# A log-sum-exp kernel on one core: another place for the last column of rows, and a transpose ahead of the last store

## The chip, the cores and the metric

The kernel runs on one core of a Trainium2 chip. A core has five engines that run their own instruction streams and wait for each other through semaphores: TensorE (PE in the profile), VectorE (DVE), ScalarE (ACT), GpSimd (POOL) and SyncE (SP). Sixteen DMA engines carry data between the chip's memory and the on-chip memory, whose 128 partitions are the rows of every tile here. The metric is the time of one execution on the device in microseconds (us); lower is better. The times before are 161.47, 161.47 and 161.59 us, with a median of 161.47 us.

## The reference

The input `x` holds 32 x 512 rows of 1024 numbers in fp32, 64 MB in all. The output is one number for each of the 16,384 rows:

```
max_x = max(x, axis=-1)
out   = max_x + log(sum(exp(x - max_x), axis=-1))
```

The kernel leaves the maximum out: it computes log(sum(exp(x))) straight away, checks on the way that no sum has left the range in which this is exact enough, and has a second, slower path with the maximum for inputs that fail this check. With the input used here the second path is jumped over.

## The kernel before

**Layout.** The 16,384 rows are spread over the 128 partitions, 128 rows to each, so a partition has 128 "columns", one per row. The columns come from two regions of the input. Columns 0 to 111 (`W` = 112) are the first 14,336 rows, and each partition has 112 rows that follow one another (`x_rows`). Columns 112 to 127 are the last 2,048 rows, 16 following rows to a partition (`x_rest`). The output is cut in the same way (`out_rows`, `out_rest`), so the last store of a partition's results writes 16 numbers, or 64 bytes, to one place.

**Stages.** The list `LOADS` says how many columns each load brings and what is done with them. SyncE issues all loads (line 143) into a ring of 48 columns; the first is 16 columns long, and toward the end they get shorter, down to 0.53 and 0.47 of a column. ScalarE applies the exponential to every load as it lands (line 235). The sums over a row are made in three ways: VectorE alone reduces whole rows (line 246); or GpSimd adds the halves of rows (line 240) and VectorE reduces the result (line 177); or, for the last loads, VectorE adds the two halves of one row and accumulates the sum in one instruction (line 256). The very last column, `LAST` = 127, is done in two pieces, "Y" and "Z", on ScalarE alone, which takes the exponential and the sum in one instruction (line 209). VectorE copies the first piece's sum into `sumexp` (line 219).

**Results.** The logarithms are ScalarE's: columns 0 to 111 at line 275, while the last loads are still coming; columns 112 to 126 at line 288; column 127 at line 290, which takes the second piece's sum and adds the first piece's as a bias. All land in the tile `res`. SyncE stores columns 0 to 111 at line 285, once the last load but one has landed, and columns 112 to 127 at line 294, once line 290 is done. This last store counts the semaphore `stored` up by 16 when it has landed.

**The check.** VectorE compares the sums with a lower bound (line 299) and the last piece's inputs with a ceiling (line 310). TensorE adds the findings up into a single number `count` (the small matmuls of lines 166, 305, 307 and 315). VectorE turns this into a truth value, `fine` (line 317), which ScalarE and VectorE each read into a register (line 321). Both then branch around the second path (line 373 is behind it), and each of them counts `done` up by one. SyncE waits for both, clears the kernel's semaphores (line 376), and ends with an instruction that waits for `stored` (line 378).

**Order.** Everything is written out by hand. Each engine executes its instructions in program order and a wait holds back all that is behind it on that engine. For this change three queues matter: SyncE's (line 285, line 294, lines 374 to 378), ScalarE's (lines 209, 288, 290, 321) and VectorE's (lines 219, 299, 310, 317, 321).

Of the kernel before, what the change touches and what calls it, by code (L numbers as in the profile page):

```python
# [16 lines left out]
B = 16  # L17
LATE = 119
AHEAD = 1
FIRST = 512  # L20


# [32 lines left out]
def kernel(  # L55
# [5 lines left out]
    nc = tc.nc  # L61
# [4 lines left out]
    P = nc.NUM_PARTITIONS  # L66
    fp32 = mybir.dt.float32
    i32 = mybir.dt.int32
    AF = mybir.ActivationFunctionType
# [3 lines left out]
    x_flat = x.flatten_outer_dims()  # L73
    n, d = x_flat.shape
    assert n % P == 0
    NC = n // P
    H = d // 2
    W = NC - B
    LAST = NC - 1
    x_rows = x_flat[0 : P * W].rearrange("(p c) d -> p (c d)", p=P)  # L80
    x_rest = x_flat[P * W : n].rearrange("(p c) d -> p (c d)", p=P)
    out_flat = out.rearrange("a b -> (a b)")
    out_rows = out_flat[0 : P * W].rearrange("(p c) -> p c", p=P)
    out_rest = out_flat[P * W : n].rearrange("(p c) -> p c", p=P)

    def source(e0, size):
        assert e0 >= W * d or e0 + size <= W * d
        return x_rest[:, e0 - W * d : e0 - W * d + size] if e0 >= W * d else x_rows[:, e0 : e0 + size]

    loads = [  # L90
        (int(size * d), [(op[0], 0 if op[0] == "Y" else int(op[1:] or 1)) for op in ops.split()])
# [5 lines left out]
    def sbuf(name, cols, dtype=fp32, rows=P):  # L97
        return nc.alloc_sbuf_tensor(name, [rows, cols], dtype).ap()

    ring = sbuf("ring", RING * d)  # L100
    sumexp = sbuf("sumexp", NC)
    res = sbuf("res", NC)
    clamped = sbuf("clamped", NC)
    bad = sbuf("bad", 3)
    over = sbuf("over", d)
# [7 lines left out]
    last_sum = nc.alloc_psum_tensor("last_sum", [P, 1], fp32).ap()  # L113
# [3 lines left out]
    act = Counted(nc, nc.scalar, "act")  # L117
    dve = Counted(nc, nc.vector, "dve")
    pe = Counted(nc, nc.tensor, "pe")
    pool = Counted(nc, nc.gpsimd, "pool")  # L120
    sp = Counted(nc, nc.sync, "early_store")
    done = nc.alloc_semaphore("done")
    again = nc.alloc_semaphore("again")
    ready = nc.alloc_semaphore("ready")
    stored = nc.alloc_semaphore("stored")
# [4 lines left out]
    dve.did(nc.vector.memset(steep, STEEP))  # L130
    less_at = dve.did(nc.vector.memset(less, -CEILING * (loads[-1][0] // 2)))


    users = []

    def load(i, here, done_before, size):
        for a, b, who, at in users:
            if a < here + size and b > here:
                sp.wait(who, at)
        users[:] = [u for u in users if not (u[0] < here + size and u[1] > here)]  # L140
        parts = [(0, FIRST), (FIRST, size)] if i == 0 else [(0, size)]
        return [
            nc.sync.dma_start(
                out=ring[:, here + a : here + b], in_=source(done_before + a, b - a)
            ).then_inc(landed[i], 16)
            for a, b in parts
        ]
# [36 lines left out]
    c = 0  # L184
    p = 0
# [6 lines left out]
    for i, (size, ops) in enumerate(loads):  # L192
        if here + size > RING * d:
            assert here == p
            p = here = 0
        if any(q < here + size and q + t * d > here for _, t, q, _ in folded):
            reduce_folded()
        dma = load(i, here, done_before, size)
        if i < AHEAD:
            first_loads.extend(x.ins for x in dma)  # L200
# [3 lines left out]
        for k, (how, s) in enumerate(ops):  # L204
            rows = ring[:, p : p + s * d].rearrange("p (c d) -> p c d", d=d)
            if how in "YZ":
# [3 lines left out]
                    out=last_exp[:, here - p : end - p], in_=ring[:, here:end], func=AF.Exp,  # L210
# [10 lines left out]
            elif how == "A":  # L221
# [3 lines left out]
                    out=v, in_=v, func=AF.Exp, accum_out=sumexp[:, c : c + 1]  # L225
# [11 lines left out]
            if how == "F":  # L237
# [3 lines left out]
                    out=rows[:, :, 0:H], in0=rows[:, :, 0:H], in1=rows[:, :, H:d], op=ALU.add  # L241
                ))
                folded.append((c, s, p, at))
            elif how == "R":
                dve.wait(act, at)
                who = (dve, dve.did(nc.vector.reduce_sum(  # L246
                    out=sumexp[:, c : c + s], in_=rows, axis=AX.X
                )))
                users.append((p, p + s * d, *who))
            elif how == "T":  # L250
# [3 lines left out]
                for r in range(s):  # L254
                    lo = rows[:, r, 0:H]
                    who = (dve, dve.did(nc.vector.scalar_tensor_tensor(  # L256
                        out=lo, in0=lo, scalar=1.0, in1=rows[:, r, H:d],
# [13 lines left out]
            if c == LATE:  # L271
# [4 lines left out]
                    out=res[:, 0:W], in_=sumexp[:, 0:W], func=AF.Ln  # L276
# [9 lines left out]

    act.wait(dve, dve.n)
    act.did(nc.scalar.activation(out=res[:, W:LAST], in_=sumexp[:, W:LAST], func=AF.Ln))  # L288
    act.wait(act, summed_by_act)
    ln_last = act.did(nc.scalar.activation(  # L290
        out=res[:, LAST:NC], in_=last_sum, func=AF.Ln, bias=sumexp[:, LAST:NC]
    ))
    sp.wait(act, ln_last)
    nc.sync.dma_start(out=out_rest, in_=res[:, W:NC]).then_inc(stored, 16)

# [2 lines left out]
        out=clamped[:, LATE:NC], in0=sumexp[:, LATE:NC], scalar=LOW,  # L300
# [10 lines left out]
        out=over[:, 0:half], in0=last_piece[:, 0:half], scalar=CEILING,  # L311
        in1=last_piece[:, half : 2 * half], op0=ALU.max, op1=ALU.max, accum_out=bad[:, 2:3],
    ))
    pe.wait(dve, dve.n)
    at = pe.did(nc.tensor.matmul(count, lhsT=bad[:, 2:3], rhs=steep, start=False, stop=True))  # L315
    dve.wait(pe, at)
    at = dve.did(nc.vector.tensor_scalar(out=fine, in0=count, scalar1=HIGH, scalar2=None, op0=ALU.is_lt))  # L317
    act.wait(dve, at)
# [8 lines left out]
            read.then_inc(done, 1)  # L327
    with nc.If(all_fine < 1):

        nc.scalar.wait_ge(sp.sem, 16)  # L330
        nc.scalar.wait_ge(stored, 16)
        rows = 0
        steps = 0
        for c0 in range(0, NC, RING):
            s = min(RING, NC - c0)
            v = ring[:, 0 : s * d].rearrange("p (c d) -> p c d", d=d)
            neg = clamped[:, c0 : c0 + s]
            if c0:
                nc.scalar.wait_ge(ready, steps)
            edge = max(c0, min(W, c0 + s))  # L340
            for c1, c2 in ((c0, edge), (edge, c0 + s)):
                if c1 == c2:
                    continue
                nc.scalar.dma_start(
                    out=ring[:, (c1 - c0) * d : (c2 - c0) * d],
                    in_=source(c1 * d, (c2 - c1) * d),
                ).then_inc(again, 16)
                rows += 16
            nc.vector.wait_ge(again, rows)
            nc.vector.tensor_reduce(  # L350
                out=neg, in_=v, op=ALU.max, axis=AX.X, negate=True
            ).then_inc(ready, 1)
            nc.vector.wait_ge(ready, steps + 1)
            nc.vector.tensor_add(
                out=v, in0=v, in1=neg[:, :, None].to_broadcast([P, s, d])
            ).then_inc(ready, 1)
            nc.scalar.wait_ge(ready, steps + 2)
            nc.scalar.activation(out=v, in_=v, func=AF.Exp).then_inc(ready, 1)
            nc.vector.wait_ge(ready, steps + 3)
            nc.vector.reduce_sum(  # L360
                out=sumexp[:, c0 : c0 + s], in_=v, axis=AX.X
            ).then_inc(ready, 1)
            steps += 4
        nc.scalar.wait_ge(ready, steps)
        nc.scalar.activation(out=res, in_=sumexp[:, 0:NC], func=AF.Ln).then_inc(ready, 1)
        nc.vector.wait_ge(ready, steps + 1)
        nc.vector.tensor_sub(out=res, in0=res, in1=clamped).then_inc(ready, 1)
        nc.scalar.wait_ge(ready, steps + 2)
        nc.scalar.dma_start(out=out_rest, in_=res[:, W:NC]).then_inc(again, 16)
        nc.scalar.dma_start(out=out_rows, in_=res[:, 0:W]).then_inc(again, 16)  # L370
        nc.scalar.wait_ge(again, rows + 32)

    nc.scalar.sem_inc(done, 1)
    nc.sync.wait_ge(done, 2)
# [2 lines left out]
    kind = dict(sync_type="semaphore", id=stored.num, ant_name="stored")  # L377
    nc.sync.add_instruction(mybir.InstEventSemaphore(
        name=nc.get_next_instruction_name(), engine=mybir.EngineType.SP,
        sync_info=mybir.SyncInfo(  # L380
            on_wait=[mybir.SyncWait(wait_mode="sem-ge-imm", wait_value=16, **kind)],
            on_update=[mybir.SyncUpdate(update_mode="sem-sub-imm", update_value=16, **kind)],
        ),
    ))

# [47 lines left out]
```

## Time and profile before

| what | value |
|---|---|
| median of the three runs | 161.47 us |
| the profiled execution's own time | 161.57 us |
| its span, from the first to the last instruction of the kernel | 160.2 us |
| time of the profiled execution outside the span | 1.37 us |
| ScalarE busy | 114.5 us (71%) |
| VectorE busy | 114.3 us (71%) |
| DMA queue of SyncE, share of 16 engines | 97.8% |
| read from memory | 67.11 MB, mean 419 GB/s |

The time outside the span is what the launch adds around the kernel. The span is what the instructions of the kernel take, and a change inside it moves the time by as much as the last instruction moves. In the rows of the profile a line "L290 ACT ACTIVATE res<-last_sum" is ScalarE's instruction of line 290, which writes `res` and reads `last_sum`; names that end in q (SPq, ACTq, DVEq) are what an engine's sequencer does by itself, such as issuing a DMA, reading a register or branching. "To landing" is the time from the issue of a DMA to its last semaphore count.

### The profile page before, as it was taken

How to read it: one execution, taken by the hardware profiler on the slowest of the kernel's cores; microseconds unless marked ns; L12 is line 12 of the kernel's file. 1: busy time of each engine (PE TensorE's matmuls, PEld its weight loads, DVE VectorE, ACT ScalarE, POOL GpSimd, SP SyncE). 2: the span in 40 equal slices, each digit the busy share in tenths (PEclk: the TensorE clock that was granted, in tenths of full speed). 3: DMA queues.
4: the chain of work that ended last, by engine and by line, in shares of the span. 5: the costliest groups of instructions: out<-in, count | busy, mean ns of one | idle time of the engine just before them, and what ended most of it. 6: DMA issues, size and time to landing. Idle time of an engine off the chain costs nothing.

```text
span 160.2 us, 221 instructions
## 1 busy us (share of the span) xinstructions
PE 2.2 (1%) x26; PEld 1.1 (1%) x26; DVE 114.3 (71%) x59; ACT 114.5 (71%) x31; POOL 37.3 (23%) x11
## 2 busy tenths in 40 slices
PE   0000000000000000000000000000000000000022
PEld 0000000000000000000000000000000000000011
DVE  0000000009999499994999859959999999999996
ACT  3000059980799708995099949992999989799996
POOL 0000000000000000000000994690004969891000
DMA  9996996996996996997999999999999999999992
GB/s 319 507 460 301 507 524 262 524 524 262 524 524 262 524 524 262 524 474 311 483 442 442 442 425 409 409 409 471 423 414 417 458 409 399 444 412 428 415 408 97
DMA packets 3025, 67.18 MB, mean 419 GB/s; under 512 B 592, under 2 KB 720, under 8 KB 1488
## 3 DMA queue, kind: packets, MB, share of 16 engines
q1 hardware_dynamic: 3024, 67.18, 97.8%
q14 instruction: 1, 0.01, 0.0%
HBM read 67.11 MB, written 0.07 MB: 419 GB/s over the span
## 4 chain that ended last, share of the span: by engine, by line
DMA 51%; ACT 28%; DVE 19%; issue 1%; PE 0%
DMA ring<-in_x_dram 51%; ACT ring L235 28%; DVE sumexp L246 16%; DVE sumexp L177 2%; DVE ring L256 1%; DVE over L310 0%; PE count L315 0%; ACT res L275 0%; DVE clamped L299 0%; DVE fine L317 0%; DVE sumexp L219 0%
## 5 line engine op out<-in xcount | busy, mean ns | idle before, releaser
L235 ACT ACTIVATE ring<-ring 128x16384 f32<-128x16384 f32 (+16 forms) x23 | 111.7, 4908 | 42.3 <-DMA ring<-in_x_dram 42.3
L246 DVE TENSOR_REDUCE sumexp<-ring 128x16 f32<-128x16384 f32 (+4 forms) x9 | 85.6, 9513 | 42.1 <-ACT ring L235 42.1
L240 POOL TENSOR_TENSOR ring<-ring 128x3072 f32<-128x3072 f32 (+3 forms) x7 | 37.1, 5315 | 107.2 <-ACT ring L235 107.2
L177 DVE TENSOR_REDUCE sumexp<-ring 128x6 f32<-128x3072 f32 (+3 forms) x7 | 18.4, 2659 | 0.0
L256 DVE SCALAR_TENSOR_TENSOR ring<-ring 128x512 f32<-128x512 f32 x15 | 9.6, 687 | 0.4 <-ACT ring L235 0.4
L127 ACT ACT_TABLE_LOAD x1 | 1.3, 1283 | 1.9 <-PEq L64 1.9
L162 PE MATMUL count<-far,bad 128*1 128x1 f32 x2 | 0.2, 164 | 153.0 <-DVE clamped L157 153.0
L166 PE MATMUL count<-sumexp,ones 128*1 128x1 f32 x18 | 1.6, 164 | 3.6 <-DVE ring L256 3.6
L128 DVE MEMSET ones<- 128x1 f32 x1 | 0.1, 59 | 2.0 <-PEq L64 2.0
L256 DVE DVE_READ_ACCUMULATOR ring<-ring 128x1 f32 x15 | 1.2, 82 | 0.0
L209 ACT ACTIVATE last_exp<-ring 128x544 f32<-128x544 f32 (+1 forms) x2 | 1.2, 588 | 0.0
L162 PEld LDWEIGHTS count<-far,bad 128*1 128x1 f32 x2 | 0.1, 82 | 153.0 <-DVE clamped L157 153.0
L166 PEld LDWEIGHTS count<-sumexp,ones 128*1 128x1 f32 x18 | 0.8, 81 | 4.4 <-DVE ring L256 4.4
L310 DVE SCALAR_TENSOR_TENSOR over<-ring 128x240 f32<-128x240 f32 x1 | 0.4, 404 | 0.0
L317 DVE TENSOR_SCALAR fine<-count 1x1 int32<-1x1 f32 x1 | 0.1, 147 | 0.3 <-PE count L315 0.3
L157 DVE SCALAR_TENSOR_TENSOR clamped<-clamped,sumexp 128x119 f32<-128x119 f32 x1 | 0.3, 283 | 0.0
L275 ACT ACTIVATE res<-sumexp 128x112 f32<-128x112 f32 x1 | 0.3, 279 | 0.0
L290 ACT ACTIVATE res<-last_sum,sumexp 128x1 f32<-128x1 f32 x1 | 0.3, 261 | 0.0
L209 ACT ACTIVATION_READ_ACCUMULATOR last_exp<-ring 128x1 f32 x2 | 0.3, 129 | 0.0
L152 DVE TENSOR_SCALAR clamped<-sumexp 128x119 f32<-128x119 f32 x1 | 0.2, 222 | 0.0
L288 ACT ACTIVATE res<-sumexp 128x15 f32<-128x15 f32 x1 | 0.2, 213 | 0.0
L299 DVE SCALAR_TENSOR_TENSOR clamped<-sumexp 128x9 f32<-128x9 f32 x1 | 0.2, 170 | 0.0
(17 smaller groups left out, 1.8 us busy)
## 6 DMA issues: line engine op xcount, KB each, us to landing
ring<-in_x_dram SPq DMA_DIRECT2D x1, 7936.0 KB, 21.3
ring<-in_x_dram SPq DMA_DIRECT2D x1, 6912.0 KB, 23.9
ring<-in_x_dram SPq DMA_DIRECT2D x1, 6400.0 KB, 19.7
ring<-in_x_dram SPq DMA_DIRECT2D x1, 4608.0 KB, 15.9
ring<-in_x_dram SPq DMA_DIRECT2D x1, 3584.0 KB, 24.0
ring<-in_x_dram SPq DMA_DIRECT2D x1, 3072.0 KB, 19.1
ring<-in_x_dram SPq DMA_DIRECT2D x1, 2288.0 KB, 24.2
ring<-in_x_dram SPq DMA_DIRECT2D x1, 1664.0 KB, 20.9
```

The source lines that it names most:

```text
L127: nc.scalar.preload_act_table_set("natural_log_exp_and_others")
L157: dve.did(nc.vector.scalar_tensor_tensor(out=clamped[:, 0:LATE], in0=clamped[:, 0:LATE], scalar=0.0, in1=sumexp[:, 0:LATE], op0=ALU.bypass ...
L162: pe.did(nc.tensor.matmul(count, lhsT=bad[:, 0:1], rhs=far, start=True, stop=False))
L166: return pe.did(nc.tensor.matmul(count, lhsT=ones, rhs=sumexp[:, c : c + 1], **kw))
L177: at = dve.did(nc.vector.reduce_sum(out=sumexp[:, c0 : c0 + s0], in_=halves, axis=AX.X))
L209: at = act.did(nc.scalar.activation(out=last_exp[:, here - p : end - p], in_=ring[:, here:end], func=AF.Exp, accum_out=first_sum if how == ...
L235: at = act.did(nc.scalar.activation(out=v, in_=v, func=AF.Exp))
L240: at = pool.did(nc.gpsimd.tensor_tensor(out=rows[:, :, 0:H], in0=rows[:, :, 0:H], in1=rows[:, :, H:d], op=ALU.add))
L246: who = (dve, dve.did(nc.vector.reduce_sum(out=sumexp[:, c : c + s], in_=rows, axis=AX.X)))
L256: who = (dve, dve.did(nc.vector.scalar_tensor_tensor(out=lo, in0=lo, scalar=1.0, in1=rows[:, r, H:d], op0=ALU.mult, op1=ALU.add, accum_out ...
L275: ln_early = act.did(nc.scalar.activation(out=res[:, 0:W], in_=sumexp[:, 0:W], func=AF.Ln))
L310: dve.did(nc.vector.scalar_tensor_tensor(out=over[:, 0:half], in0=last_piece[:, 0:half], scalar=CEILING, in1=last_piece[:, half : 2 * half ...
```

## The change

The columns now come from three regions of the input. Columns 0 to 111 are where they were. Columns 112 to 126 are 15 following rows to each partition. Column 127 is the last 128 rows of the input, one for each partition, side by side (`x_last`). The loads keep their sizes; the two pieces of the last column now start 4 KB apart from partition to partition, where they were 64 KB apart, and the other pieces of the tail 60 KB.

The store at the end becomes two. The first, of columns 112 to 126, is 60 bytes from each of the 128 partitions; SyncE issues it after the logarithms of line 288. For column 127 the logarithm goes into the first column of a new tile `turn` (128 x 32), whose other columns GpSimd sets to zero at the start. VectorE then transposes each block of 32 x 32 into `turned`. Partitions 0, 32, 64 and 96 of `turned` now hold 32 results each in a row, and SyncE stores these four rows of 128 bytes. VectorE waits for line 290 before the transpose, which stands ahead of line 317 in its queue. `stored` counts to 32.

In the second path, which isn't executed here, the loads and stores follow the three regions, and two waits are moved from ScalarE to VectorE.

```
@@
+SQUARE = 32
@@
-    x_rest = x_flat[P * W : n].rearrange("(p c) d -> p (c d)", p=P)
+    x_rest = x_flat[P * W : P * LAST].rearrange("(p c) d -> p (c d)", p=P)
+    x_last = x_flat[P * LAST : n]
@@
-    out_rest = out_flat[P * W : n].rearrange("(p c) -> p c", p=P)
+    out_rest = out_flat[P * W : P * LAST].rearrange("(p c) -> p c", p=P)
+    out_last = out_flat[P * LAST : n]
 
     def source(e0, size):
-        assert e0 >= W * d or e0 + size <= W * d
-        return x_rest[:, e0 - W * d : e0 - W * d + size] if e0 >= W * d else x_rows[:, e0 : e0 + size]
+        for c0, c1, rows in ((0, W, x_rows), (W, LAST, x_rest), (LAST, NC, x_last)):
+            if c0 * d <= e0 < c1 * d:
+                assert e0 + size <= c1 * d
+                return rows[:, e0 - c0 * d : e0 - c0 * d + size]
@@
+    turn = sbuf("turn", SQUARE)
+    turned = sbuf("turned", SQUARE)
@@
+    pool.did(nc.gpsimd.memset(turn, 0.0))
@@
     act.did(nc.scalar.activation(out=res[:, W:LAST], in_=sumexp[:, W:LAST], func=AF.Ln))
+    sp.wait(act, act.n)
+    nc.sync.dma_start(out=out_rest, in_=res[:, W:LAST]).then_inc(stored, 16)
     act.wait(act, summed_by_act)
     ln_last = act.did(nc.scalar.activation(
-        out=res[:, LAST:NC], in_=last_sum, func=AF.Ln, bias=sumexp[:, LAST:NC]
+        out=turn[:, 0:1], in_=last_sum, func=AF.Ln, bias=sumexp[:, LAST:NC]
     ))
-    sp.wait(act, ln_last)
-    nc.sync.dma_start(out=out_rest, in_=res[:, W:NC]).then_inc(stored, 16)
@@
     at = pe.did(nc.tensor.matmul(count, lhsT=bad[:, 2:3], rhs=steep, start=False, stop=True))
+    dve.wait(act, ln_last)
+    row = dve.did(nc.vector.transpose(out=turned, in_=turn))
+    sp.wait(dve, row)
+    nc.sync.dma_start(
+        out=out_last.rearrange("(b q) -> b q", q=SQUARE), in_=turned[0:P:SQUARE, :]
+    ).then_inc(stored, 16)
     dve.wait(pe, at)
     at = dve.did(nc.vector.tensor_scalar(out=fine, in0=count, scalar1=HIGH, scalar2=None, op0=ALU.is_lt))
...
-            on_wait=[mybir.SyncWait(wait_mode="sem-ge-imm", wait_value=16, **kind)],
-            on_update=[mybir.SyncUpdate(update_mode="sem-sub-imm", update_value=16, **kind)],
+            on_wait=[mybir.SyncWait(wait_mode="sem-ge-imm", wait_value=32, **kind)],
+            on_update=[mybir.SyncUpdate(update_mode="sem-sub-imm", update_value=32, **kind)],
```

More of the change, by code (lines that the diff above doesn't have):

```diff
@@ L328 @@
     with nc.If(all_fine < 1):
-        nc.scalar.wait_ge(sp.sem, 16)
-        nc.scalar.wait_ge(stored, 16)
+        nc.vector.wait_ge(sp.sem, 16)
+        nc.vector.wait_ge(stored, 32)
         rows = 0
@@ L339 @@
                 nc.scalar.wait_ge(ready, steps)
-            edge = max(c0, min(W, c0 + s))
-            for c1, c2 in ((c0, edge), (edge, c0 + s)):
+            edges = [max(c0, min(e, c0 + s)) for e in (0, W, LAST, NC)]
+            for c1, c2 in zip(edges, edges[1:]):
                 if c1 == c2:
@@ L368 @@
         nc.scalar.wait_ge(ready, steps + 2)
-        nc.scalar.dma_start(out=out_rest, in_=res[:, W:NC]).then_inc(again, 16)
+        nc.scalar.dma_start(out=out_last[:, None], in_=res[:, LAST:NC]).then_inc(again, 16)
+        nc.scalar.dma_start(out=out_rest, in_=res[:, W:LAST]).then_inc(again, 16)
         nc.scalar.dma_start(out=out_rows, in_=res[:, 0:W]).then_inc(again, 16)
-        nc.scalar.wait_ge(again, rows + 32)
+        nc.scalar.wait_ge(again, rows + 48)
     nc.scalar.sem_inc(done, 1)
```

## The prediction

> **What bounds the kernel now.** I read the page's chain first, then SyncE's waits, and then the last four microseconds in order of time, because the change leaves the first 157 us alone but for the addresses of the tail's loads.
>
> ```profile
> span 160.2 us, 221 instructions
> ...
> DMA 51%; ACT 28%; DVE 19%; issue 1%; PE 0%
> ```
>
> The body is a stream of loads. The windows of the tail show how the DMA engines and ScalarE stand to each other there (the last two columns are the DMA share and GB/s):
>
> ```profile
> 80.00:100.00 20.00, 0.00 (x0) 0.00 (x0) 17.76 (x2) 17.61 (x3) 9.97 (x1) 1.00 1.00 433
> ...
> 138.00:142.00 4.00, 0.00 (x0) 0.00 (x0) 4.00 (x2) 3.94 (x3) 3.29 (x2) 1.00 0.99 426
> 142.00:146.00 4.00, 0.00 (x0) 0.00 (x0) 4.00 (x3) 4.00 (x2) 2.73 (x2) 1.00 0.99 423
> 146.00:150.00 4.00, 0.00 (x0) 0.00 (x0) 4.00 (x9) 4.00 (x2) 0.00 (x0) 1.00 0.99 418
> 150.00:154.00 4.00, 0.38 (x4) 0.17 (x4) 3.57 (x14) 4.00 (x4) 0.00 (x0) 1.00 1.00 413
> ```
>
> From 142 us on ScalarE is busy 4.00 of every 4.00 us and the DMA engines are too: the two are in step. A faster tail of loads would gain next to nothing, since ScalarE has no gap to close; a slower one would cost its loss in full. The end, from the last exponential on, in order of time:
>
> ```profile
> 157.25 0.61 ACT L209 ACTIVATE last_exp<-ring 128x544 f32<-128x544 f32 x1
> 157.26 0.35 SPq L285 DMA_DIRECT2D out_dram<-res  x1
> ...
> 157.99 0.15 DVE L219 COPY sumexp<-first_sum 128x1 f32<-128x1 f32 x1
> ...
> 158.18 0.17 DVE L299 SCALAR_TENSOR_TENSOR clamped<-sumexp 128x9 f32<-128x9 f32 x1
> ...
> 158.28 0.40 DVE L310 SCALAR_TENSOR_TENSOR over<-ring 128x240 f32<-128x240 f32 x1
> ...
> 158.39 0.21 ACT L288 ACTIVATE res<-sumexp 128x15 f32<-128x15 f32 x1
> ...
> 158.51 0.26 ACT L290 ACTIVATE res<-last_sum,sumexp 128x1 f32<-128x1 f32 x1
> 158.60 0.08 DVE L310 DVE_READ_ACCUMULATOR over<-ring 128x1 f32 x1
> ...
> 158.74 0.19 PE L315 MATMUL count<-steep,bad 128*1 128x1 f32 x2
> 158.79 0.34 SPq L294 DMA_DIRECT2D out_dram<-res  x1
> 158.97 0.15 DVE L317 TENSOR_SCALAR fine<-count 1x1 int32<-1x1 f32 x1 [0.28 <-PE count L315]
> ```
>
> Two paths run from here to the end of the span. One is the store: line 290 ends at 158.77, SyncE issues at 158.79. The other is the check: line 317, the register reads, the branches. The views of the sequencers' lines and SyncE's waits say which is last:
>
> ```profile
> L321 ACTq TENSOR_LOAD <-fine x1: 467/467/467, 159.1 to 159.1; - x1
> ...
> L373 ACTq EVENT_SEMAPHORE  x1: 17/17/17, 159.8 to 159.8; - x1
> ...
> L376 SPq EVENT_SEMAPHORE_RANGE_CLEAR  x1: 71/71/71, 159.8 to 159.8; - x1
> ...
> L378 SPq EVENT_SEMAPHORE  x1: 17/17/17, 160.2 to 160.2; - x1
> ...
> SPq L376 <- ACTq L373: 0.7, 1, 0.7
> SPq L378 <- SPq L378: 0.3, 1, 0.3
> ```
>
> After the check SyncE clears the semaphores at 159.8 and then still waits 0.3 us at line 378, for the store. So the landing of the last store ends the span, and the check is 0.3 us earlier. The chain view ends in line 317 because it follows engines, not this landing; SyncE's own waits decide.
>
> **The store, taken apart.** The row of the issue, and the DMA in the stretch 159.5 to 160.2 (40 slices of 0.0175 us) and, for the early store, 158.0 to 158.5 (slices of 0.0125 us):
>
> ```profile
> out_dram<-res SPq DMA_DIRECT2D x1, 56.0 KB, 1.6
> ...
> out_dram<-res SPq DMA_DIRECT2D x1, 8.0 KB, 1.4
> ...
> GB/s 0 0 0 0 0 0 0 4 44 66 70 48 55 55 52 26 30 15 7 0 0 0 0 0 0 0 0 0 0 0 0 0 0 0 0 0 0 0 0 0
> DMA packets 144, 0.01 MB, mean 12 GB/s; under 512 B 144, under 2 KB 144, under 8 KB 144
> ...
> GB/s 0 0 0 0 0 0 0 0 36 143 72 179 179 215 215 215 287 287 287 358 179 287 287 217 179 180 215 180 108 143 36 72 36 0 0 0 0 0 0 0
> ```
>
> The last store's packets (128 of data and 16 that count the semaphore) run from 159.5 + 7 x 0.0175 = 159.62 to 159.5 + 19 x 0.0175 = 159.83. So of its 1.4 us 0.83 pass from issue to the first packet, 0.21 are the train of packets, and 0.37 pass until the last count. The early store starts its packets at 158.0 + 8 x 0.0125 = 158.10, which is 0.84 after its issue at 157.26: the time to the first packet is the same for 448 bytes a partition as for 64.
>
> **The change, part by part.**
>
> Loads. Sizes, order and ring are the same; only addresses change (60 KB and 4 KB between partitions for 64 KB). The 20 us rows show 433 GB/s at 448 KB between partitions and the tail 426 to 413 at 64 KB, falling with the size of the pieces, at a DMA share of 0.99 to 1.00: the engines' own pace shows, not the addresses. I take 0. What covers a loss: nothing, ScalarE follows the landings directly. Bounds: the tail is 157.3 - 138.0 = 19.3 us, so a pace 1% higher gives at most some 0.05 us, and 1% lower costs 0.19 us.
>
> GpSimd's clearing of `turn`: one instruction at the start. The waits show that GpSimd then has 87.4 us to spare before its first addition, which covers it:
>
> ```profile
> POOL ring L240 <- ACT ring L235: 107.2, 5, 87.4
> ```
>
> Cost 0; without that cover it would be one small instruction, some 0.1 us (an estimate from the 0.15 of the copy of one column, above).
>
> Store of columns 112 to 126 (call it A). SyncE issues it when line 288 is done, 158.39 + 0.21 + 0.02 = 158.62 (0.02 is the step from line 290's end to SyncE's issue). It holds SyncE for 0.34, to 158.96. It lands 1.4 later like the 64-byte store, at 160.02, or 1.6 later like the early one, at 160.22. Cost on the path: nothing so far.
>
> Transpose. VectorE waits for line 290 (158.77 + 0.02 = 158.79); the queue ahead of it (line 310) is done at 158.68. The trace has no transpose. From below the nearest row is the copy of 128x1, 0.15 us; from above the pass over 128x240, 0.40. 32 columns lie much nearer the first: the pass over 128x9 takes 0.17, and I take 0.20. Done at 158.99. Behind it in VectorE's queue stands line 317, which would start at 159.0 instead of 158.97, as its matmuls are done at 158.74 + 0.19 = 158.93. ScalarE's and VectorE's register reads, both branches and line 376 follow, each 0.05 later: 159.9 instead of 159.8. Its cover is the 0.3 us that SyncE waits at line 378. Were the cover gone, the 0.05 would count.
>
> Store of column 127 (call it B). SyncE waits for VectorE: 158.99 + 0.02 = 159.01 against 158.79, so 0.22 later. SyncE has just issued A. Loads that are issued directly behind another are held longer than one that came after a wait:
>
> ```profile
> L143 SPq DMA_DIRECT2D ring<-in_x_dram x1: 328/328/328, 126.5 to 126.5; - x1
> ...
> L143 SPq DMA_DIRECT2D ring<-in_x_dram x3: 434/443/485, 126.8 to 127.8; - x3
> ```
>
> That is 0.1 us more, and B comes 0.05 behind A's issue, so some of it applies: I take 0.05, with bounds of 0 and 0.1 (0.16 by the longest). Then B has 4 packets of data, on at most four of the 16 DMA engines. Its time to the first packet I take as 0.83, by both stores. Its train of 0.21 shrinks to about 0.03 (at most 4 + 16 = 20 of the 144 packets, at the same pace), the last count is 0.37 behind: 0.83 + 0.03 + 0.37 = 1.23. The bounds: 1.4 if the train doesn't matter, 1.6 by the early store, and from below 0.9, if preparing 128 pieces is what half of the 0.49 between the end of the 0.34 issue and the first packet goes into, with some of the issue.
>
> The sum for B: 159.01 + 0.05 + 1.23 = 160.29 against 160.2, and since the 1.4 and 160.2 are rounded (158.79 + 0.83 + 0.21 + 0.37 = 160.20), the difference is +0.09 us. Written as terms: transpose and its two handovers +0.22, issue behind issue +0.05, shorter train -0.18. A's landing (160.02 to 160.22) and the check (159.9) stay under it. The profiled execution took 161.57, so its like would take 161.66; the median of the three runs is 0.10 under the profiled one, so I put 161.47 + 0.09 = 161.56 us.
>
> A rule weighed. The trace gives a train of 0.21 us to 144 packets. The Trainium skill (DMA: Bandwidth & Descriptors, "Anatomy of one DMA") puts most of a DMA's cost into a constant, chiefly the receipt of the write, with only a term of bytes beside it. By that rule four packets would save nothing that 8 KB didn't already: the sum would be without the -0.18. The trace agrees that most of the 1.4 is constant (0.83 + 0.37), but shows the train beside it. The same page's section on why a semaphore counts 16 says that a DMA on few engines counts only these after its data and the rest at once; no row here shows such a DMA.
>
> **The rivals.**
>
> *The store's time is constant.* B lands 1.41 after its issue whatever its packets. For it: 56 KB and 8 KB differ by 0.2 only. Against it: half of those 0.2 are the difference of the trains, 25 slices or 0.31 us against 12 slices or 0.21. Time: 161.47 + 0.22 + 0.05 = 161.74; with a transpose of 0.25 or more and the full 0.1 behind A it is over 161.8. This is the page's rule above.
>
> *B starts sooner too.* Fewer pieces to prepare shorten the 0.83. From 1.23 - 0.09 = 1.14 on, the kernel is faster. At 0.95 B lands at 160.01 and the time is 161.47 - 0.19 = 161.28. It can't go much beyond: the check ends at 159.9 + 0.07 and A lands at 160.02 at the earliest. Against it: both stores took 0.83 to 0.84 to the first packet, but both have 128 pieces.
>
> *Store A is last.* Pieces of 60 bytes lie across the multiples of 64 in the output, and two neighbours share the 64 bytes between them, where each piece had its own before. It decides when A takes over 160.29 - 158.62 = 1.67 us to land, and makes the kernel measurably slower (160.2 + 0.32) from 1.9 us on; at 2.0 it gives 161.47 + 0.42 = 161.89. For it: no row has such pieces. Against it: of the two stores shown, the one of smaller pieces is the quicker.
>
> *The loads suffer.* The last column is one stretch of 512 KB that all DMA engines read together. 2% over the tail's 19.3 us cost 0.39: 161.95. Only the last two loads have 4 KB between partitions; 60 KB for 64 KB is a small step. Against it the DMA share near 1.00 at an even pace over two different spacings.
>
> *A slow transpose.* At 0.40 B lands 0.20 later than summed, 161.76, and line 317 ends 0.2 later, still covered.
>
> **How the numbers follow.** About 0.2%, 0.32 us, is what a measurement of this kernel can tell from no change, so "within" means 161.15 to 161.79. My sum has a chance of 0.44, with a range of its own of 161.42 to 161.68. The constant store: 0.18, of which 0.05 are over 161.79. B sooner: 0.14, of which 0.04 reach beyond 0.2% with the scatter of the runs, as the check's end caps the gain at some 0.25. Store A last: 0.10, of which 0.09 slower. Loads: 0.09, of which 0.07 slower and 0.02 faster. Slow transpose: 0.05, of which 0.02 slower. That makes 0.06 faster, 0.71 within and 0.23 slower. The range takes in the low end of B and most of the slower cases: 161.28 to 161.95.
>
> **What the profile after would show.** A transpose on VectorE at 158.79 of about 0.20; two issues of SyncE, at 158.62 and 159.01 to 159.06, the second 0.34 to 0.44 long; landings of 1.4 and 1.23; line 376 at 159.9 and line 378 at 160.29, still waiting for B; line 209 at 157.25 as before. Line 209 later than 157.3 means the loads suffer; a first landing over 1.67 means A is last; a second landing at 1.4 means that the packets don't count. Wrong would be most of all the assumption that B's time to the first packet is that of a store from 128 partitions.

## The result, and the profile after

The changed kernel takes 161.96 us (median of nine runs, 161.93 to 162.21) against 161.52 (161.47 to 161.67) for the kernel before, measured with it: a ratio of 1.0029, with a 95% interval of 1.0018 to 1.0039. It is 0.44 us slower; 161.56 had been forecast, with a range up to 161.95.

The profiled execution took 162.21, the most of the nine. Some of that was there before any changed address was in use: the first load, whose place in the input is the old one, landed after 21.5 us where it had taken 21.3. In the runs below, with the same start, it landed after 21.3 to 21.5.

```profile
span 160.8 us, 224 instructions
...
ring<-in_x_dram SPq DMA_DIRECT2D x1, 7936.0 KB, 21.5
```

The two ends are therefore compared from the last logarithm on, line 302 of the changed kernel. In order of time:

```profile
157.41 0.61 ACT L219 ACTIVATE last_exp<-ring 128x544 f32<-128x544 f32 x1
...
158.55 0.21 ACT L298 ACTIVATE res<-sumexp 128x15 f32<-128x15 f32 x1
...
158.66 0.26 ACT L302 ACTIVATE turn<-last_sum,sumexp 128x1 f32<-128x1 f32 x1
...
158.78 0.34 SPq L300 DMA_DIRECT2D out_dram<-res  x1
...
158.95 0.21 DVE L327 STREAM_TRANSPOSE turned<-turn 128x32 f32<-128x32 f32 x1
159.13 0.15 DVE L333 TENSOR_SCALAR fine<-count 1x1 int32<-1x1 f32 x1
159.19 0.63 SPq L329 DMA_DIRECT2D out_dram<-turned  x1
```

The logarithm ends at 158.92. The transpose takes 0.21 and SyncE issues store B at 159.19, 0.27 behind the logarithm; before it was 0.02. Then the issue of B holds SyncE for 0.63, where both stores of the kernel before took 0.34 or 0.35. The sequencers' lines:

```profile
L393 SPq EVENT_SEMAPHORE_RANGE_CLEAR  x1: 71/71/71, 160.0 to 160.0; - x1
...
L395 SPq EVENT_SEMAPHORE  x1: 17/17/17, 160.8 to 160.8; - x1
```

and SyncE's waits:

```profile
SPq L395 <- SPq L395: 0.8, 1, 0.8
```

SyncE is done with the check at 160.0 and now waits 0.8 us for the store, where it waited 0.3. From the logarithm to the last instruction 160.8 - 158.92 = 1.9 us pass, against 160.2 - 158.77 = 1.4 before: with the rounding this is the 0.44 of the medians. The DMA from 159.5 to 160.9 (40 slices of 0.035 us):

```profile
GB/s 0 0 0 17 58 49 50 33 12 2 0 0 0 0 0 0 0 0 0 0 0 0 0 0 0 0 11 4 0 0 0 0 0 0 0 0 0 0 0 0
DMA packets 152, 0.01 MB, mean 6 GB/s; under 512 B 152, under 2 KB 152, under 8 KB 152
```

Store A's train runs from slice 3 to 9, 159.60 to 159.85. B has the other 8 of the 152 packets (4 of data and, if they are counted as A's are, 4 for the semaphore), where up to 20 had been forecast. Its train is two slices long, 0.07 us for the 0.03 forecast, but it begins at slice 26, 159.5 + 26 x 0.035 = 160.41: 1.22 after its issue, where the store before needed 0.83.

### The profile page after: what moved, and what is told of

It is laid out like the page before. It is cut to its first block, busy times and chain, and to the rows that moved or that the text cites. A ratio compares the mean times of both kernels' runs of the same rounds, so it can differ in the third digit from the quotient of the medians.

```text
span 160.8 us, 224 instructions
## 1 busy us (share of the span) xinstructions
PE 2.2 (1%) x26; PEld 1.1 (1%) x26; DVE 114.4 (71%) x60; ACT 114.5 (71%) x31; POOL 37.4 (23%) x12
## 4 chain that ended last, share of the span: by engine, by line
DMA 51%; ACT 29%; DVE 18%; issue 0%
DMA ring<-in_x_dram 51%; ACT ring L245 28%; DVE sumexp L256 15%; DVE sumexp L187 2%; ACT last_exp L219 1%; DVE turned L327 0%; ACT res L285 0%; ACT turn L302 0%; ACT res L298 0%; DVE fine L333 0%
## 6 DMA issues: line engine op xcount, KB each, us to landing
ring<-in_x_dram SPq DMA_DIRECT2D x1, 7936.0 KB, 21.5
```

## The experiments

Three theories could say why B is slow. *Queue*: it stands directly behind store A. *Few rows*: a store from 4 partitions is slow to issue. *Stride*: its four partitions do not lie next to each other but 32 apart. Times are medians; beside each stands the kernel before, run with it.

**B ahead of A.**

```
-    sp.wait(act, act.n)
-    nc.sync.dma_start(out=out_rest, in_=res[:, W:LAST]).then_inc(stored, 16)
...
     sp.wait(dve, row)
     nc.sync.dma_start(out=out_last..., in_=turned[0:P:SQUARE, :]).then_inc(stored, 16)
+    nc.sync.dma_start(out=out_rest, in_=res[:, W:LAST]).then_inc(stored, 16)
```

> Changed: SyncE issues the 4-packet store of column 127 first and the store of columns 112 to 126 behind it. In the changed kernel the 4-packet store held SyncE for 0.63 us and landed 1.62 us after its issue. Theory few rows (a store from 4 partitions is itself slow to issue): the 4-packet store still takes about 0.63 us to issue; the other follows at about 159.8 and lands near 161.3, so the kernel takes about 162.4. Theory queue (it was slow because it stood directly behind another store): its issue takes 0.34, the other store's 0.43 to 0.49, and the kernel takes about 162.1.

Measured: 162.51 us against 161.52. SyncE's issues in order of time:

```profile
158.97 0.64 SPq L327 DMA_DIRECT2D out_dram<-turned  x1
159.65 0.39 SPq L330 DMA_DIRECT2D out_dram<-res  x1
```

With nothing ahead of it but a store whose issue ended 1.4 us earlier, B still takes 0.64. So the queue isn't what makes B slow. Store A, now directly behind B, takes 0.39 where it took 0.34.

**Other rows for B.** First 16 adjacent partitions, then 4 adjacent ones; the transpose and all waits stay.

```
-    out=out_last.rearrange("(b q) -> b q", q=SQUARE), in_=turned[0:P:SQUARE, :]
+    out=out_last.rearrange("(b q) -> b q", q=8), in_=turned[0:16, 0:8]         # 16 rows
+    out=out_last.rearrange("(b q) -> b q", q=SQUARE), in_=turned[0:4, :]       # 4 rows
```

> Changed: the last store takes 16 adjacent partitions with 8 numbers each (16 packets of 32 bytes) in place of 4 partitions with 32; column 127's results are then not the right ones, the work and its waits are the same. Theory few rows, if fewer than 16 rows are what costs: issue of 0.43 to 0.49, landing about 1.3 after it, time about 161.6. Theory queue: issue of 0.63, time 161.95. Theory stride (rows 32 partitions apart cost): like few rows.

> Changed: the last store takes the 4 adjacent partitions 0 to 3 in place of 0, 32, 64 and 96; column 127's results are then not the right ones, the work and its waits are the same. Theory few rows and theory queue: issue of 0.63 and time of 161.95, as the changed kernel. Theory stride: issue of 0.43 to 0.49 and time about 161.6.

Measured: 161.76 us for the 16 rows (ratio 1.0015, 1.0005 to 1.0025) and 161.59 for the 4 adjacent ones (1.0004, 0.9995 to 1.0014), both against 161.52. With 16 rows, SyncE's issue in order of time, the DMA of 159.9 to 160.6 (slices of 0.0175 us), the line of its last instruction, and store A with its time to landing:

```profile
159.21 0.41 SPq L329 DMA_DIRECT2D out_dram<-turned  x1
```

```profile
GB/s 0 0 0 0 0 0 0 0 0 0 0 2 10 2 0 6 4 4 2 2 0 0 0 0 0 0 0 0 0 0 0 0 0 0 0 0 0 0 0 0
```

```profile
L395 SPq EVENT_SEMAPHORE  x1: 17/17/17, 160.6 to 160.6; - x1
```

```profile
out_dram<-res SPq DMA_DIRECT2D x1, 7.5 KB, 1.4
```

With 4 adjacent rows, the issue, the DMA of 159.4 to 160.1 (store A's train first, then B's), and the last instruction:

```profile
159.01 0.35 SPq L329 DMA_DIRECT2D out_dram<-turned  x1
```

```profile
GB/s 0 0 10 45 72 52 53 48 52 42 32 21 11 7 0 0 0 0 0 0 0 0 15 0 8 0 8 0 0 0 0 0 0 0 0 0 0 0 0 0
```

```profile
L395 SPq EVENT_SEMAPHORE  x1: 17/17/17, 160.2 to 160.2; - x1
```

Four adjacent rows are issued in 0.35 us, directly behind A (0.43 to 0.49 had been expected), their first packet comes 159.4 + 22 x 0.0175 - 159.01 = 0.78 after the issue, and they land 160.2 - 159.0 = 1.2 after it. The rows in the output, the bytes and the number of pieces are those of the changed kernel, where the first packet took 1.22. So neither few rows nor the queue is the cause; the stride between the partitions is. Without it the changed kernel is level with the kernel before. The 16 rows missed the 161.6 that was expected of them: they land in 160.6 - 159.2 = 1.4, like 128. Their train is shorter (8 slices, 0.14 us, for 0.21), but their issue takes 0.41 and their first packet comes 159.9 + 11 x 0.0175 - 159.21 = 0.88 after it. What made the 4 rows quicker is thus not the shorter train alone.

**The same on the kernel before.** Its last store cut to four partitions, 32 apart or adjacent, without a transpose and with nothing ahead on SyncE.

```
-    nc.sync.dma_start(out=out_rest, in_=res[:, W:NC]).then_inc(stored, 16)
+    nc.sync.dma_start(out=out_rest[0:P:32, :], in_=res[0:P:32, W:NC]).then_inc(stored, 16)   # 32 apart
+    nc.sync.dma_start(out=out_rest[0:4, :], in_=res[0:4, W:NC]).then_inc(stored, 16)         # adjacent
```

> Changed: the kernel before, with its last store cut to partitions 0, 32, 64 and 96 (4 packets of 64 bytes; the other partitions' results of columns 112 to 127 are left out). No transpose, nothing directly ahead of the store on SyncE. Theory few rows: issue of 0.63 instead of 0.34, landing about 1.6 after it instead of 1.4, time about 161.7. Theory queue: issue of 0.34, landing about 1.2, time about 161.35.

> Changed: the kernel before, its last store cut to the 4 adjacent partitions 0 to 3 (4 packets of 64 bytes; the rest of columns 112 to 127 is left out), with nothing directly ahead of it on SyncE. The 4 partitions that lie 32 apart took 0.63 us to issue at this place. Theory stride: issue of 0.34 to 0.36, landing 1.18 after it, time 161.3. Theory few rows: 0.63 and 161.77, as with 32 apart.

Measured: 161.77 us against 161.56 for 32 apart (1.0013, 1.0003 to 1.0022), 161.38 against 161.59 for the adjacent ones (0.9985, 0.9975 to 0.9994). SyncE's issue and the DMA of the stretch 159.9 to 160.6 for 32 apart, in slices of 0.0175 us:

```profile
158.88 0.63 SPq L294 DMA_DIRECT2D out_dram<-res  x1
```

```profile
GB/s 0 0 0 0 0 0 0 0 0 0 0 0 8 4 4 0 0 0 0 0 0 0 0 0 0 0 0 0 0 0 0 0 0 0 0 0 0 0 0 0
```

For the adjacent ones the issue, the DMA of 159.4 to 160.1, and the last of SyncE's waits:

```profile
158.82 0.34 SPq L294 DMA_DIRECT2D out_dram<-res  x1
```

```profile
GB/s 0 0 0 0 0 0 0 0 0 0 8 0 4 4 0 0 0 0 0 0 0 0 0 0 0 0 0 0 0 0 0 0 0 0 0 0 0 0 0 0
```

```profile
SPq L376 <- ACTq L373: 0.7, 1, 0.7
```

The first packet comes 159.9 + 12 x 0.0175 - 158.88 = 1.23 after the issue in the one case and 159.4 + 10 x 0.0175 - 158.82 = 0.76 in the other. The stride costs 0.47 us here, 0.29 of it while SyncE issues and the rest before the first packet. In the adjacent case SyncE's wait for the store has gone from the list (its wait for ScalarE's branch is the last of it): the check no longer ends ahead of the store, so a still quicker store would gain nothing.

**Other strides.**

```
+    nc.sync.dma_start(out=out_rest[0:8:2, :], in_=res[0:8:2, W:NC]).then_inc(stored, 16)       # 4 rows, step 2
+    nc.sync.dma_start(out=out_rest[0:128:8, :], in_=res[0:128:8, W:NC]).then_inc(stored, 16)   # 16 rows, step 8
+    nc.sync.dma_start(out=out_rest[0:128:2, :], in_=res[0:128:2, W:NC]).then_inc(stored, 16)   # 64 rows, step 2
```

> Changed: as the cut store of 4 partitions, but partitions 0, 2, 4 and 6. If any step between partitions costs the sequencer: issue of 0.63. If only steps that leave a group of 32 partitions do: 0.35.

> Changed: the last store cut to 16 partitions, 0, 8, ... 120. If a step costs a fixed amount: issue of 0.63. If it costs per partition, 0.28 / 4 = 0.07 each: 0.34 + 16 x 0.07 = 1.5. If the step is dear only when fewer than 16 rows are stored: 0.35 to 0.41.

> Changed: the last store cut to every second partition, 64 of them. If a step costs a fixed amount: issue of 0.63. If per partition, 0.07 each: 0.34 + 64 x 0.07 = 4.8. If only with fewer than 16 rows: 0.35 to 0.41.

Measured in one execution each: 161.84, 161.76 and 161.83 us, against 161.59. The issue's row of the three in this order, each with its DMA in slices of 0.0175 us (from 159.9 for the first, from 159.6 for the others):

```profile
158.75 0.74 SPq L294 DMA_DIRECT2D out_dram<-res  x1
```

```profile
GB/s 0 0 0 0 0 0 0 0 0 0 8 4 0 4 0 0 0 0 0 0 0 0 0 0 0 0 0 0 0 0 0 0 0 0 0 0 0 0 0 0
```

```profile
158.66 0.55 SPq L294 DMA_DIRECT2D out_dram<-res  x1
```

```profile
GB/s 0 0 0 0 0 0 0 0 0 0 0 0 0 0 0 19 8 4 8 8 4 8 0 4 0 0 0 0 0 0 0 0 0 0 0 0 0 0 0 0
```

```profile
158.73 0.55 SPq L294 DMA_DIRECT2D out_dram<-res  x1
```

```profile
GB/s 0 0 0 0 0 0 0 0 0 0 0 0 0 0 0 0 0 0 22 48 30 15 29 30 26 15 11 7 4 0 0 0 0 0 0 0 0 0 0 0
```

Each of the steps tried, 2, 8 and 32, costs between 0.2 and 0.4 us of issue, and the cost is not per partition: 64 rows take no longer than 16. It isn't quite a fixed amount either, which would have been 0.63 in all three. The first packets come 1.3, 1.2 and 1.2 after the issue, where the stores of 4, 16 and 128 adjacent rows needed 0.76 to 0.92. Why a step costs anything, and why 4 rows take longer than 16 or 64, stays open. In these cut stores the rows in the output are as far apart as the partitions, so a step on that side is tried along with the other; store B's rows lie side by side in the output, and B costs 0.63 all the same, so a step between the partitions is enough.

**The transpose alone.** The kernel before, with its old store waiting for a transpose.

```
+    pool.did(nc.gpsimd.memset(turn, 0.0))
...
-    sp.wait(act, ln_last)
-    nc.sync.dma_start(out=out_rest, in_=res[:, W:NC]).then_inc(stored, 16)
...
     at = pe.did(nc.tensor.matmul(count, lhsT=bad[:, 2:3], rhs=steep, start=False, stop=True))
+    dve.wait(act, ln_last)
+    row = dve.did(nc.vector.transpose(out=turned, in_=turn))
+    sp.wait(dve, row)
+    nc.sync.dma_start(out=out_rest, in_=res[:, W:NC]).then_inc(stored, 16)
```

> Changed: the kernel before with the transpose alone: VectorE waits for the last logarithm and transposes a tile (of zeros), and SyncE waits for that before it issues the old store of 128 pieces of 64 bytes. The sum put the transpose and its handovers at 0.22 us, the changed kernel's rows at 0.25; if that adds up, the time is that of before plus 0.25, near 161.8, with an issue of 0.34 and a landing 1.4 after it. If the check behind the transpose were the end, line 378's wait would be gone.

Measured: 161.78 us against 161.55, 0.23 more (1.0017, 1.0008 to 1.0026). In order of time, and SyncE's last wait:

```profile
158.40 0.26 ACT L293 ACTIVATE res<-last_sum,sumexp 128x1 f32<-128x1 f32 x1
...
158.69 0.21 DVE L318 STREAM_TRANSPOSE turned<-turn 128x32 f32<-128x32 f32 x1
...
158.93 0.34 SPq L320 DMA_DIRECT2D out_dram<-res  x1
```

```profile
SPq L383 <- SPq L383: 0.6, 1, 0.6
```

The issue stands 158.93 - 158.66 = 0.27 behind the logarithm, as in the changed kernel. SyncE's last wait, for the store, is longer than before (0.6 for 0.3), so the check behind the transpose keeps its cover.

**The input's places alone.**

```
-    x_rest = x_flat[P * W : n].rearrange("(p c) d -> p (c d)", p=P)
+    x_last = x_flat[P * LAST : n]
+    x_rest = x_flat[P * W : P * LAST].rearrange("(p c) d -> p (c d)", p=P)
...
```

The three dots stand for the lines of `source`, which become those of the changed kernel, and for the loads of the second path.

> Changed: the kernel before with the changed kernel's input places alone (60 KB and 4 KB between partitions in the tail); the stores are those of before, so results of the last 2048 rows come out at other places than the reference's. If the addresses cost nothing, the time is that of before within 0.1 us. If the later first landing in the changed kernel's profile (0.15 us) is of the addresses, it is 0.15 us slower.

Measured: 161.59 us against 161.56, a ratio of 1.0002 (0.9993 to 1.0011). The addresses cost nothing that can be told, and the later start of the profiled execution above was not theirs.

**No transpose: 128 pieces of 4 bytes.**

```
-    dve.wait(act, ln_last)
-    row = dve.did(nc.vector.transpose(out=turned, in_=turn))
-    sp.wait(dve, row)
-    nc.sync.dma_start(out=out_last..., in_=turned[0:P:SQUARE, :]).then_inc(stored, 16)
+    sp.wait(act, ln_last)
+    nc.sync.dma_start(out=out_last[:, None], in_=turn[:, 0:1]).then_inc(stored, 16)
```

> Changed: no transpose; column 127 is stored straight from the first column of turn, 128 pieces of 4 bytes from 128 partitions, directly behind the store of columns 112 to 126. Theory few rows: the issue falls to 0.43 to 0.49, the landing to about 1.4 to 1.5 after it; with the issue at about 158.98 to 159.02 that is 160.4 to 160.5 and a time of 161.7 to 161.8. Theory queue: the issue stays at 0.63 and the time is 161.8 to 161.9, only the 0.25 of the transpose less the 0.2 of the longer train better than the changed kernel.

Measured: 167.65 us against 161.52. The issue was as expected of few rows, 0.43; the landing was not. The issue in order of time, SyncE's last wait, the DMA's row with its time to landing, and the DMA of 159.4 to 160.4 (slices of 0.025 us):

```profile
159.06 0.43 SPq L327 DMA_DIRECT2D out_dram<-turn  x1
```

```profile
SPq L391 <- SPq L391: 6.1, 1, 6.1
```

```profile
out_dram<-turn SPq DMA_DIRECT2D x1, 0.5 KB, 7.0
```

```profile
GB/s 0 0 0 0 14 60 55 47 53 39 24 15 3 0 0 0 0 0 0 0 0 0 0 1 4 5 4 4 3 2 1 0 0 0 0 0 0 0 0 0
```

The second train, that of column 127, is over at slice 30, 159.4 + 31 x 0.025 = 160.18, and SyncE's wait ends at 166.1. So nearly 6 of the 7.0 us pass after the last packet: the end of a train of packets doesn't tell when the store has landed.

To see whether it was the size of the pieces or their neighbourhood, the kernel before got a last store of column 127 alone, at its old places 64 bytes apart:

```
-    nc.sync.dma_start(out=out_rest, in_=res[:, W:NC]).then_inc(stored, 16)
+    nc.sync.dma_start(out=out_rest[:, B - 1 : B], in_=res[:, LAST:NC], allow_slow_non_contiguous=True).then_inc(stored, 16)
```

> Changed: the kernel before, its last store cut to column 127: 128 pieces of 4 bytes that lie 64 bytes apart in the output (columns 112 to 126 are left out). Side by side such pieces took 7.0 us to land. If it is the neighbours within one stretch of 64 bytes that hold each other up, it lands in about 1.4; if 4-byte pieces are slow by themselves, in about 7.

Measured: 161.57 us against 161.45, one execution each. Its landing, as the view of the line has it:

```profile
DMA to landing us min/median/max: 1.4/1.4/1.4
```

Pieces of 4 bytes land in 1.4 us when they lie 64 bytes apart and in 7.0 when they lie side by side. (The two kernels also differ in the tile that is read and in the store ahead, which itself landed in 1.4 us.) The Trainium skill (DMA: Bandwidth & Descriptors, "Specifications") says that transfers below 512 bytes make the DMA read, modify and write. A small size alone doesn't show here. That it is the neighbours is the likeliest reading of two kernels and not shown alone; how near a neighbour has to be was not tried.

## Why the prediction was wrong

*The loads, cost 0:* right, by the run with the input's places alone.

*Store A, no cost on the path:* right. Its issue took 0.34 at 158.78, and pieces of 60 bytes side by side held nothing up: the same store landed 1.4 after its issue in the run with 16 rows, which from 158.78 is 160.2, ahead of the end at 160.8. This rival is out.

*The transpose and its handovers, +0.22:* nearly right. The instruction took 0.21 for the 0.20 forecast, the handovers somewhat more, +0.25 in the rows and +0.23 in the run with the transpose alone. The check behind it kept its cover: SyncE cleared the semaphores 160.0 - 158.92 = 1.1 after the logarithm, against 159.8 - 158.77 = 1.0 before, still well ahead of the store.

*Issue behind issue, +0.05:* wrong by as much for this pair. Four partitions 32 apart took 0.63 with A ahead of them and 0.63 to 0.64 without; four adjacent rows took 0.35 directly behind A. Stores of more rows did show such an addition: 0.39, 0.41 and 0.43 directly behind another, in the runs with A behind B, with 16 rows and without the transpose, against 0.34.

*Shorter train, -0.18:* near. B's train took 0.07 for 0.21 before, which is -0.14. Four adjacent rows land 1.2 after the issue instead of 1.4, some 0.2 less, but 0.05 of that is an earlier first packet that the sum hadn't put there. And 16 rows gain nothing, so the count of packets that the step went by is not all of it.

*B's time to the first packet, taken as 0.83 "by both stores":* this is the step that failed, the one that the prediction named as its weakest. It is 1.22, because the four rows of a transposed tile lie 32 partitions apart. Both stores of the kernel before read all 128 partitions in a row, so its profile held no DMA with a step between partitions, and the bounds were looked for in the wrong property, the number of pieces. With the rows adjacent, the kernel came out at 161.59, within 0.03 of the forecast 161.56. Part of that is luck: the issue and the first packet came cheaper than summed by some 0.05 each, the transpose and the train dearer by 0.03 and 0.06. The stride adds the other 161.96 - 161.59 = 0.37 by the medians, and 0.47 by the rows of the cut stores.

*The rivals.* In time the suffering loads (161.95) and store A as the last (161.89) came nearest to 161.96, and by luck: both are out, as shown above, so the upper end of the range stood near the result for a cost that wasn't there. *The store's time is constant* (161.74 to over 161.8) had its own reason wrong too: with adjacent rows the landing did fall to 1.2. On the rule behind it, that a DMA's cost is a constant and a term of bytes: at equal bytes the time moved from 1.2 to 1.6 with the placing of the rows. The section that the prediction names for this rule (the Trainium skill, DMA: Bandwidth & Descriptors, "Anatomy of one DMA") is about DMAs that GpSimd issues; those here are SyncE's. *B sooner* happened in part with adjacent rows (0.76 for 0.83), and the check's end capped it, as said there.

The sum by the rows is now: transpose +0.25, B's landing 1.6 for 1.4, together some +0.45, against +0.44 measured.

Of the versions tried, none that computes the whole output beats the kernel before. The transpose costs 0.23; the 0.2 that four adjacent rows give back only make up for it, and a transpose in blocks of 32 x 32 doesn't leave them adjacent.

## What to carry to other kernels

Price a DMA by the shape of its access on the chip, not only by its bytes and packets: here a step between partitions cost 0.2 to 0.4 us of issue and put the first packet 0.3 to 0.6 us later, with 4, 16 and 64 rows. Four adjacent rows in place of 128 were worth 0.2 us at the end of this kernel (16 rows weren't), which one more small instruction with its two handovers, 0.23 us, uses up. And where a new operation has a property that no row of the profile shares (a stride, a single partition), that property is where the range should be widest.

## What the runs showed of the hardware that was not expected

A store from 4 partitions was issued in 0.34 to 0.35 us when they were adjacent, 0.63 to 0.64 when 32 apart and 0.74 when 2 apart; 16 partitions 8 apart and 64 partitions 2 apart took 0.55. A store of 128 pieces of 4 bytes side by side took 7.0 us to land, nearly 6 of them after its last packet, against 1.4 with the pieces 64 bytes apart, while pieces of 60 bytes side by side landed in 1.4 too.
